# The experts' numbers ahead of the tokens' weights, and another ending of the expert sum, in a transformer block with sixteen experts

## The chip, the cores and the metric

The kernel runs on one core of a Trainium2 chip. The core has five engines with a queue of instructions each: PE (matmul), DVE (vector), ACT (scalar), POOL (GpSimd) and SP, which here only issues DMAs. PE writes to PSUM, the others work between PSUM and SBUF, and 16 DMA engines move data between SBUF and HBM. The metric is the device time of one execution in microseconds.

## The reference

One block: a token mixer (mLSTM heads and a Fourier part), then a mixture of experts with a norm and a residual around it. What the change touches is the end of it.

```python
x = x + gate1 * rmsnorm(y, g_post_mix)
h2 = modulate(rmsnorm(x, g_pre_ffn), shift2, scale2)
x = x + gate2 * rmsnorm(hier_moe(h2), g_post_ffn)

# hier_moe: 512 tokens, 16 experts, each token goes to 2 of one group of 4
for e in range(16):
    a = silu(h @ w_gate[e]) * (h @ w_up[e])
    y = y + combine[..., e, None] * (a @ w_down[e])
```

Tokens have 1024 features, an expert 512 inner ones; everything is float32.

## The kernel before

The mixer takes the first 300 us or so. Then each expert is one column: a list of its tokens is made, the tokens' rows are gathered from a DRAM buffer `h2d`, gate, up and down are applied, the weighted result `yo` is added into the DRAM buffer `ybuf` by an indirect scatter on POOL's queue (L1580). There are 16 columns in the order `SEQ = [0, 1, 2, 11, 3, 8, 4, 12, 5, 9, 6, 13, 7, 10, 14, 15]`. Columns 0 to 2, 14 and 15 hold fixed experts; the eleven between them (3 to 13) are ranked by their number of tokens at run time, so their weights are loaded from an address that SP reads from a small array `idi` of experts' numbers (`values_load`, L1811). `idi` is made on DVE within the routing (L1683 to L1688), behind the first column's code. The routing also makes the tokens' weights in three bf16 parts (L1650 to L1655), sums them by matmuls (`lw`, `lq`) and writes the lists' indices (L1417).

A column takes 12 raw weight tiles of 128x1024 (0.5 MB each), loaded by SP at L1306: 8 for gate and up in four parts, 4 for down. There are 21 raw buffers in rotation (`next_raw`). A heavy column (up to 128 tokens) splits each raw tile in two: ACT casts it to fp32r (`hi`, L1328), DVE takes the rest (`lo`, L1329), and three products hi*hi, lo*hi and hi*lo follow on PE, so 6 matmuls of 128x512 per tile; there are 5 pairs of hi and lo. The raw buffer is free when DVE has its rest. A light column (32 or 64 tokens) multiplies the raw tiles in plain fp32.

`position(n, wsrc)` writes column `SEQ[n]`: `gate_up` with its four parts, and between the parts (the list `mid`) the transposes of the column before, then the turning of the next column's tokens; behind it the `down` of the column before (for the last position, the down of column 14 stands within gate and up, behind part 1). Columns 13, 14, 15 below are named by their place from the end: third from last is column 10 (64 tokens, light), then 14 and 15, heavy both. The prediction calls the third from last "column 13", after its position n = 13.

The ending, `finish(True)`, has three jobs. `ybuf` holds everything but the results of the last two columns, which stay in PSUM (`py`). Each of four blocks of 128 tokens is read from `ybuf` (L1841, on SP), squared and summed on ACT (L1852), multiplied with the gate row `G2` on POOL (704 of 1024 features, L1853) and DVE (L1854), and written to `out` (`w`, L1862 and L1863); tokens of the last two lists are left at the residual there by a zero factor `rest`. For these two lists, rows of `ybuf` are gathered (L1817), the PSUM results are added (`l`, L1870), normed (`p`, L1877), and added into `out` by an indirect scatter (`o`, L1883). A mean square goes through a power on POOL (L1848). `t0` is the down of the last column in three products per tile. The helper `after` chains instructions of one engine in the order of the code, so the order of the ending is that of a string:

```python
ORDER = "s0 s3 w0 t0 s2 l0 w3 s1 w2 w1 l1 p0 p1 o0 o1".split()
```

Elsewhere a scheduler sets the order on each engine, by priorities that follow the code. The helper `mm` at L213 records all matmuls, so PE's rows are told apart by the name of the tile that they write.

## Time and profile before

| | us |
|---|---|
| median of 3 runs | 650.36 (648.5 to 650.47) |
| the profiled execution | 645.57 |
| its span | 643.4 |
| PE busy | 549.3 (85%) |
| DVE busy | 375.3 (58%) |
| ACT busy | 294.8 (46%) |
| POOL busy | 228.0 (35%) |
| DMA moved | 165.24 MB, 257 GB/s in the mean |

The span is the time from the first to the last instruction of the program, the device time also holds what lies around it. Times within rows are us from the span's start, a row of the timeline gives start and duration, and in brackets how long the engine stood idle ahead of it and what ended that. Rows that several instructions share have their count behind an x; back-to-back instructions of one engine overlap by a little, so a row's duration divided by the count is their distance. A row of the stretches gives, behind the stretch and its length, the busy time and the instruction count of PE, PE's weight loads, DVE, ACT and POOL, then the granted PE clock, the busy share of the DMA engines and GB/s.

### The profile page before, as it was taken

The page shows a single profiled execution, that of the slowest core. Times are in us where ns is not written, and L with a number is a line of the kernel's source. Part 1 is how long each engine was busy: PE and PEld are TensorE (multiplying, and loading weights), DVE is VectorE, ACT ScalarE, POOL GpSimd, SP SyncE. Part 2 cuts the span into 40 slices and gives each one's busy share as a digit, 9 for nine tenths or more (in the row PEclk, how much of TensorE's full clock was granted, in tenths as well). Part 3 has the DMA queues.
Part 4 walks back from the last instruction along what each step waited for, and adds up shares of the span by engine and source line. Part 5 has one row for each costly group of instructions (what it writes and reads, how often), then busy time and mean ns, then how long its engine had stood idle before and what let it go on. Part 6 is the DMA issues. An engine that isn't in the chain of part 4 may idle for free. (4 is left out here: it accounts for less than half of the span.)

```text
span 643.4 us, 9141 instructions
## 1 busy us (share of the span) xinstructions
PE 549.3 (85%) x3073; PEld 378.1 (59%) x3073; DVE 375.3 (58%) x692; ACT 294.8 (46%) x478; POOL 228.0 (35%) x264
## 2 busy tenths in 40 slices
PE   3789979699999869997799999999998988998650
PEld 1256855688565647874677766566654555465430
DVE  3560794836247663428999998452735445366780
ACT  2560635443134335224386765462725345367630
POOL 8343940076033346536442236113120010001672
PEclk9989998899999989998799999999999999999875
DMA  8965601131699774256676899999999999998331
GB/s 265 389 253 195 232 0 51 31 99 50 214 318 318 255 310 164 92 189 264 215 275 237 288 387 376 333 389 384 376 389 390 379 387 379 399 383 324 139 132 25
DMA packets 58390, 165.24 MB, mean 257 GB/s; under 512 B 9305, under 2 KB 16757, under 8 KB 58340
## 3 DMA queue, kind: packets, MB, share of 16 engines
q1 hardware_dynamic: 50244, 154.07, 64.2%
q0 software_dynamic: 5536, 10.08, 6.5%
q10 hardware_dynamic: 2560, 0.47, 0.4%
q8 instruction: 25, 0.41, 0.2%
q14 instruction: 25, 0.20, 0.1%
HBM read 154.92 MB, written 15.02 MB: 264 GB/s over the span
## 5 line engine op out<-in xcount | busy, mean ns | idle before, releaser
L1329 DVE TENSOR_TENSOR U<-U,U 128x1024 fp32r<-128x1024 f32 x118 | 141.7, 1248 | 33.8 <-ACT U L1328 33.3
L1328 ACT CAST U<-U 128x1024 fp32r<-128x1024 f32 x118 | 118.4, 1051 | 19.5 <-PE y L213 5.3
L213 PE MATMUL y<-U,U 128*128 128x512 f32 x368 | 100.4, 410 | 10.6 <-ACT U L1510 4.3
L213 PEld LDWEIGHTS y<-U,U 128*128 128x128 f32 x368 | 68.6, 193 | 29.5 <-ACT U L1510 4.5
L213 PE MATMUL gate<-U,U 128*128 128x512 f32 x186 | 55.8, 401 | 5.0 <-DVE U L1329 2.5
L213 PE MATMUL up<-U,U 128*128 128x512 f32 x188 | 56.5, 400 | 1.7 <-ACT U L1328 1.7
L213 PE MATMUL uz<-U,U 128*128 128x512 f32 x192 | 52.4, 409 | 0.2 <-ACT U L603 0.2
L216 POOL TENSOR_TENSOR U<-U,U 128x512 fp32r<-128x512 f32 (+2 forms) x32 | 43.3, 1371 | 4.1 <-ACT U L812 1.5
L213 PEld LDWEIGHTS gate<-U,U 128*128 128x128 f32 x186 | 34.0, 189 | 16.2 <-ACT U L1328 4.8
L213 PEld LDWEIGHTS up<-U,U 128*128 128x128 f32 x188 | 35.0, 189 | 12.1 <-ACT U L1328 3.2
L213 PEld LDWEIGHTS uz<-U,U 128*128 128x128 f32 x192 | 34.9, 189 | 11.9 <-issue 5.5
L213 PE MATMUL gul<-U,U 128*32 128x256 f32 (+1 forms) x296 | 40.4, 442 | 0.0
L1580 POOL DMA_INDIRECT ybuf<-U x8 | 13.9, 1737 | 69.3 <-ACT U L1556 31.6
L1580 POOL DMA_INDIRECT ybuf<-U,U x7 | 11.4, 1628 | 65.5 <-ACT U L1560 47.4
L1335 POOL DMA_INDIRECT U<-h2d,U x16 | 17.6, 1099 | 46.0 <-PE xet L1363 20.4
L213 PE MATMUL win<-U,U 128*128 128x512 f32 x96 | 25.1, 408 | 0.0
L216 DVE TENSOR_TENSOR U<-U,U 128x512 fp32r<-128x512 f32 (+1 forms) x18 | 16.2, 921 | 13.9 <-POOL U L216 9.9
L1490 DVE TENSOR_TENSOR U<-U,up 128x512 f32<-128x512 f32 x10 | 6.9, 686 | 29.8 <-PE up L213 29.8
L1366 DVE TENSOR_TENSOR U<-xet,U 128x512 fp32r<-128x512 f32 x18 | 12.1, 687 | 19.8 <-ACT U L1365 19.8
L213 PEld LDWEIGHTS gul<-U,U 128*32 128x32 f32 (+1 forms) x296 | 14.0, 117 | 15.2 <-issue 9.6
L428 ACT CAST U<-U 128x512 fp32r<-128x512 f32 (+2 forms) x30 | 21.1, 763 | 3.7 <-DMA U<-in_w_in_dram 3.7
L213 PE MATMUL yl<-U,U 128*32 128x256 f32 (+1 forms) x156 | 21.8, 448 | 0.0
(439 smaller groups left out, 1055.7 us busy)
## 6 DMA issues: line engine op xcount, KB each, us to landing
U<-in_w_gate_dram SPq DMA_DIRECT2D x64, 512.0 KB
U<-in_w_up_dram SPq DMA_DIRECT2D x64, 512.0 KB
U<-in_w_down_dram SPq DMA_DIRECT2D x64, 512.0 KB
U<-in_w_ada_dram SPq DMA_DIRECT2D x48, 512.0 KB
U<-in_w_in_dram SPq DMA_DIRECT2D x6, 1024.0 KB
U<-in_w_out_dram SPq DMA_DIRECT2D x4, 1024.0 KB
U<-in_x_dram SPq DMA_DIRECT2D x4, 512.0 KB
x0d<-U SPq DMA_DIRECT2D x4, 512.0 KB
```

The lines of the kernel that those rows point to most:

```text
L213: PE.matmul(out=o, lhsT=l, rhs=r, start=start, stop=stop)
L216: (eng or V).tensor_tensor(o, a, b, op=OP.subtract)
L428: S.copy(hi[:, s], raw[:, s])
L1328: after(S, lambda: S.copy(hi.ap, r.ap))
L1329: after(V, lambda: V.tensor_tensor(lo.ap, r.ap, hi.ap.bitcast(F32), op=OP.subtract))
L1335: g = G.indirect_dma_start(out=xe[0:n], out_offset=None, in_=h2d[:, :], in_offset=bass.IndirectOffsetOnAxis(ap=gi[0:n], axis=0), bounds_ch ...
L1366: V.tensor_tensor(xl[:, s], tp, xh[:, s].bitcast(F32), op=OP.subtract)
L1490: run["mul"] = V.tensor_tensor(sg.ap, sg.ap, p2[1], op=OP.mult)
L1580: run["scatter"] = G.indirect_dma_start(out=to, out_offset=bass.IndirectOffsetOnAxis(ap=gi, axis=0), in_=yo[:, 0:n], in_offset=None, bound ...
```

## The change

It has four parts.

1. In the routing, the instructions that make `idi` stand ahead of those that make the tokens' weights. SP's first register loads of `idi` move with it.
2. The down of the third column from the end is written behind part 1 of column 14's gate and up, not behind all of it. Its four weight loads on SP stand ahead of column 14's parts 2 and 3.
3. The ending begins within the last column: behind part 2 `setup` takes 14 raw buffers, loads `G2`, reads the four blocks of `ybuf`, now on POOL's queue, and gathers the rows of the last two lists; behind part 3 `first` scales two blocks. The multiplication with `G2` is whole on DVE.
4. The last down is in plain fp32 from the raw tiles: one copy of the transposed activations, no splits, 8 matmuls for 24. Then come two more blocks, four writes, and each of the last two lists with its scatter at once behind it. A list's result is multiplied with `G2` while the power is made, and with the power's result afterwards, half on ACT and half on DVE.

```diff
@@ routing, behind the first column
     with tc.issue_after(listed.ins):
-        for w in rw:
-            w()
-        wp, wr_ = ...
-        (the tokens' weights in three bf16 parts, the matmuls lw, parts_sum into ls[:, :, 2])
...
         V.tensor_tensor(ohr, gcol(rank), grow(iota[:, 0:NDYN]), op=OP.is_equal)
-        V.tensor_tensor(t3, ..., op=OP.mult)
-        V.tensor_reduce(lsd, t3, axis=AX.X, op=OP.add)
-        indices(NPRE, NPRE + NDYN, lsd)
         V.tensor_copy(idf, ids)
         V.tensor_tensor(t3[:, :, 0, :], ohr, gcol(ids[:, D_]), op=OP.mult)
         V.tensor_reduce(idf[:, D_], t3[:, :, 0, :], axis=AX.X, op=OP.add)
         idi = idb.ap.bitcast(I32)
         V.tensor_copy(idi, idf)
+        for w in rw:
+            w()
+        wp, wr_ = ...
+        (the same as above)
+        V.tensor_tensor(t3, ..., op=OP.mult)
+        V.tensor_reduce(lsd, t3, axis=AX.X, op=OP.add)
+        indices(NPRE, NPRE + NDYN, lsd)
@@ position(n, wsrc)
         if n == NE - 1:
             mid[1] = lambda: run.update(py=down(pend, box["ya"], keep=True))
+            mid[2:] = [run["setup"], run["first"]]
...
+        if n == NE - 2:
+            mid[1] = lambda: (ahead(), down(pend, box["ya"]))
         s_ = gate_up(tiles, wsrc, run["xs"], mid)
-        if pend is not None and n < NE - 1:
+        if pend is not None and n < NE - 2:
             down(pend, box["ya"], mid=ahead if SEQ[n + 1] == STAR else None)
@@ the ending: new functions, called from position or behind the loop
+    def setup(part):
+        g2 = next_raw()
+        SP.dma_start(out=g2.ap, in_=bc(g2d[:, :], [128, 1024]))
+        fin.update(G2=g2.ap, junk=next_raw(), ys=[next_raw() for _ in range(4)], zs=[next_raw() for _ in range(4)])
+        eng = G if part else SP
+        for tt in range(4):
+            line[eng] = eng.dma_start(out=fin["ys"][tt].ap, in_=ybuf[tt * 128:(tt + 1) * 128, :])
+        if part:
+            fin.update(yg=[next_raw() for _ in LAST], zg=[next_raw() for _ in LAST])
+            for yg, p in zip(fin["yg"], LAST):
+                after(G, lambda: gather(yg.ap, ybuf, iiv[:, p:p + 1], T))
+    def scale(tt, part):
+        y1, y2, c = fin["ys"][tt], fin["zs"][tt], 44 + 4 * tt
+        after(S, lambda: S.activation(fin["junk"].ap, y1.ap, AF.Square, accum_out=st[:, c:c + 1]))
+        inv(c)
+        after(V, lambda: V.tensor_tensor(y2.ap, y1.ap, fin["G2"], op=OP.mult))
...
-            after(G, lambda: G.tensor_tensor(y2[:, 0:NPG], y1[:, 0:NPG], G2[:, 0:NPG], op=OP.mult))
-            after(V, lambda: V.tensor_tensor(y2[:, NPG:1024], y1[:, NPG:1024], G2[:, NPG:1024], op=OP.mult))
...
     def last(i):
...
+        after(V, lambda: V.tensor_tensor(zg.ap, yg.ap, fin["G2"], op=OP.mult))
+    def put(i):
+        zg, r = fin["zg"][i], st[:, 25 + 4 * i:26 + 4 * i]
+        after(S, lambda: S.mul(zg[:, 0:512], zg[:, 0:512], r))
+        after(V, lambda: V.tensor_scalar(zg[:, 512:1024], zg[:, 512:1024], r, None, op0=OP.mult))
+        after(G, lambda: G.indirect_dma_start(out=outv, ..., in_=zg.ap, ..., compute_op=OP.add))
+    def last_products(raws):
+        sg = run["pend"][2][0][0]
+        tp = pT("at")
+        for q in range(4):
+            PE.transpose(tp[:, q * 128:(q + 1) * 128], sg[:, q * 128:(q + 1) * 128], ident)
+        after(S, lambda: S.copy(sg.ap, tp))
+        y = pA("y0"), pA("y1")
+        for kk in range(4):
+            for n in range(2):
+                mm(y[n], sg[:, kk * 128:kk * 128 + 128], raws[kk][:, n * 512:n * 512 + 512], kk == 0, kk == 3)
+        py.append(y)
+    def first():
+        py.append(run["py"])
+        for tt in range(2):
+            scale(tt, True)
@@ behind the last position
-    ahead_of = gate()
-    units = [unit(run["pend"][1], 2, kk) for kk in range(4)]
-    finish(True)      (walks ORDER = "s0 s3 w0 t0 s2 l0 w3 s1 w2 w1 l1 p0 p1 o0 o1")
+    raws = [raw_unit(run["pend"][1], 2, kk) for kk in range(4)]
+    line.update({V: run["mul"], S: run["silu"]})
+    last_products(raws)
+    for tt in range(2, 4):
+        scale(tt, True)
+    for tt in range(4):
+        write(tt)
+    last(0)
+    put(0)
+    last(1)
+    put(1)
```

Line numbers of the changed kernel are two lower than before at the helpers (L1327 for L1329), and differ by more within the routing and the ending.

Part 1 on DVE. Before, in the routing behind the first column (`U_99` is a slot with the routing's small arrays, `lq`, `dup` are PSUM tiles of lists), the cast of the numbers is the last row:

```order
L1679 TENSOR_TENSOR U_99<-U_99 128x363
L1742 COPY U_75<-U_99 128x16
L1366 TENSOR_TENSOR U_1004<-xet,U_2005 128x512
L1681 TENSOR_REDUCE U_99<-U_99 128x33
L1728 COPY U_99<-lq 128x11x2
L1417 SCALAR_TENSOR_TENSOR U_99<-U_99 128x11
L1684 TENSOR_TENSOR U_99<-U_99,U_81 128x11x11
L1707 COPY U_99<-dup 128x9
L1685 TENSOR_REDUCE U_99<-U_99 128x11
L1708 TENSOR_TENSOR U_99<-U_99 128x3
L1644 TENSOR_REDUCE U_99<-lq 128x11
L1688 CAST U_81<-U_99 128x16
```

In the changed kernel the cast is the seventh of these rows, and the 128x1024 row behind it is the split of a raw tile that stood at 333.61 in the trace before:

```order
L1665 TENSOR_TENSOR U_99<-U_99,U_81 128x11x11
L1129 TENSOR_TENSOR U_99<-U_99 128x8
L1415 SCALAR_TENSOR_TENSOR U_99<-U_99 128x2
L1666 TENSOR_REDUCE U_99<-U_99 128x11
L1130 TENSOR_TENSOR U_99<-U_99 128x8
L1741 TENSOR_TENSOR U_99<-U_99 128x16
L1669 CAST U_81<-U_99 128x16
L1131 TENSOR_REDUCE U_99<-U_99 128x2
L1134 SCALAR_TENSOR_TENSOR U_99<-U_99 128x2
L1128 TENSOR_REDUCE U_99<-U_99 128x2
L1327 TENSOR_TENSOR U_1845<-U_1831,U_2425 128x1024
```

The cast stands 35 rows earlier; the index rows of 128x11 (L1417 before, L1415 now) stay behind the tokens' weights.

Part 2 on ACT. Before, at column 14: two casts of its part 1 (the first two rows), its four casts of parts 2 and 3, its silu, the copy of its transposed activations, the light down's result (`yl`), and the casts of column 15.

```order
L1328 CAST U_2425<-U_2421 128x1024
L1328 CAST U_1004<-U_99 128x1024
L1328 CAST U_2005<-U_2427 128x1024
L1328 CAST U_1845<-U_2427 128x1024
L1328 CAST U_2425<-U_2426 128x1024
L1328 CAST U_2425<-U_75 128x1024
L1489 ACTIVATE U_1831<-gate 128x512
L1510 CAST U_1004<-at 128x512
L1556 ACTIVATE U_99<-yl,U_99 128x512
L1328 CAST U_1004<-U_1831 128x1024
L1328 CAST U_2005<-U_81 128x1024
L1328 CAST U_1845<-U_2426 128x1024
```

Now the result of the light down stands ahead of the four casts of parts 2 and 3 (the four rows behind it), and one cast of column 15 ahead of the silu:

```order
L1326 CAST U_2425<-U_2421 128x1024
L1326 CAST U_1004<-U_99 128x1024
L1554 ACTIVATE U_99<-yl,U_99 128x512
L1326 CAST U_2005<-U_1831 128x1024
L1326 CAST U_1845<-U_2006 128x1024
L1326 CAST U_2425<-U_99 128x1024
L1326 CAST U_2425<-U_2427 128x1024
L1326 CAST U_1004<-U_1831 128x1024
L1487 ACTIVATE U_1831<-gate 128x512
L1326 CAST U_2005<-U_81 128x1024
L1326 CAST U_1845<-U_2426 128x1024
L1508 CAST U_1004<-at 128x512
```

What moved is the row with `yl`, from behind the silu to the middle of column 14; all casts of parts 2 and 3 now stand behind it on ACT.

Part 4 on POOL, where the last instructions are. Before, powers and products of the blocks, the power of the last list, and both scatters (`out_dram`) together at the end:

```order
L1848 TENSOR_TENSOR U_75<-U_75 128x1
L1853 TENSOR_TENSOR U_2006<-U_2427,U_99 128x704
L1848 TENSOR_TENSOR U_75<-U_75 128x1
L1858 TENSOR_TENSOR U_75<-U_75,U_99 128x1
L1848 TENSOR_TENSOR U_75<-U_75 128x1
L1883 DMA out_dram<-U_99 512x1024
L1883 DMA out_dram<-U_1831,U_99 512x1024
```

Now the first list's scatter stands between the two lists' powers, and the products with `G2` are gone:

```order
L1832 TENSOR_TENSOR U_75<-U_75 128x1
L1841 TENSOR_TENSOR U_75<-U_75,U_99 128x1
L1832 TENSOR_TENSOR U_75<-U_75 128x1
L1841 TENSOR_TENSOR U_75<-U_75,U_99 128x1
L1832 TENSOR_TENSOR U_75<-U_75 128x1
L1863 DMA out_dram<-U_81,U_99 512x1024
L1832 TENSOR_TENSOR U_75<-U_75 128x1
L1863 DMA out_dram<-U_2426,U_99 512x1024
```

The four reads of `ybuf` stand on this queue as well, ahead of the two gathers, behind the last scatter into `ybuf`.

More of the change, by code (lines that the diff above doesn't have):

```diff
@@ L49 @@
 NXE = 3
-NPG = 704
 RT = 1616
-ORDER = "s0 s3 w0 t0 s2 l0 w3 s1 w2 w1 l1 p0 p1 o0 o1".split()
 NU = 2
@@ L1804, in dyn_w, with gather @@
         return src
+    LAST = NE - 2, NE - 1
+    outv = out.rearrange("o t c -> (o t) c")
+    fin = {}
+    def gather(dst, src, idx, rows):
+        return G.indirect_dma_start(out=dst, out_offset=None, in_=src[:, :], in_offset=bass.IndirectOffsetOnAxis(ap=idx, axis=0),
+                                    bounds_check=rows - 1, oob_is_err=False)
+    def setup(part):
[9 more added lines that the diff above has]
+                after(G, lambda: gather(yg.ap, ybuf, iiv[:, p:p + 1], T))
@@ new lines, in inv @@
+    def inv(c):
+        after(V, lambda: V.tensor_scalar(st[:, c + 2:c + 3], st[:, c:c + 1], 1.0 / D, EPS, op0=OP.mult, op1=OP.add))
+        after(G, lambda: G.tensor_tensor(st[:, c + 1:c + 2], st[:, c + 2:c + 3], mhalf[:, 0:1], op=OP.pow))
+    def scale(tt, part):
[3 more added lines that the diff above has]
+        after(V, lambda: V.tensor_tensor(y2.ap, y1.ap, fin["G2"], op=OP.mult))
+        if part:
+            after(G, lambda: G.tensor_tensor(st[:, c + 1:c + 2], st[:, c + 1:c + 2], rest[:, tt:tt + 1], op=OP.mult))
@@ new lines, in write, with last @@
+    def write(tt):
+        y2 = fin["zs"][tt].ap
+        after(V, lambda: V.scalar_tensor_tensor(y2, y2, st[:, 45 + 4 * tt:46 + 4 * tt], x1[tt].ap, op0=OP.mult, op1=OP.add))
+        after(SP, lambda: SP.dma_start(out=outv[tt * 128:(tt + 1) * 128, :], in_=y2))
+    def last(i):
+        yg, zg, w, c = fin["yg"][i], fin["zg"][i], lists_of(LAST[i])[1], 24 + 4 * i
+        for n in range(2):
+            s = slice(n * 512, n * 512 + 512)
+            after(V, lambda: V.scalar_tensor_tensor(yg[:, s], py[i][n], w, yg[:, s], op0=OP.mult, op1=OP.add))
+            after(S, lambda: S.activation(fin["junk"][:, s], yg[:, s], AF.Square, accum_out=st[:, c + 3 * n:c + 3 * n + 1]))
+        after(V, lambda: V.tensor_tensor(st[:, c:c + 1], st[:, c:c + 1], st[:, c + 3:c + 4], op=OP.add))
+        inv(c)
+        after(V, lambda: V.tensor_tensor(zg.ap, yg.ap, fin["G2"], op=OP.mult))
@@ new lines, in put @@
+    def put(i):
+        zg, r = fin["zg"][i], st[:, 25 + 4 * i:26 + 4 * i]
+        after(S, lambda: S.mul(zg[:, 0:512], zg[:, 0:512], r))
+        after(V, lambda: V.tensor_scalar(zg[:, 512:1024], zg[:, 512:1024], r, None, op0=OP.mult))
+        after(G, lambda: G.indirect_dma_start(out=outv, out_offset=bass.IndirectOffsetOnAxis(ap=iiv[:, LAST[i]:LAST[i] + 1], axis=0),
+                                              in_=zg.ap, in_offset=None, bounds_check=T - 1, oob_is_err=False, compute_op=OP.add))
@@ new lines, in last_products @@
+    def last_products(raws):
[6 more added lines that the diff above has]
+        for kk in range(4):
+            for n in range(2):
+                mm(y[n], sg[:, kk * 128:kk * 128 + 128], raws[kk][:, n * 512:n * 512 + 512], kk == 0, kk == 3)
+        py.append(y)
+    py = []
+    def first():
+        py.append(run["py"])
+        for tt in range(2):
+            scale(tt, True)
@@ L1806, in body @@
+    run.update(setup=lambda: setup(True), first=first)
     for n in range(NPRE, NE):
@@ L1811, in body @@
             position(n, dyn_w(nc.values_load(idi[0:1, c:c + 1], engines=(mybir.EngineType.SP,), min_val=0, max_val=NE - 1)))
-    LAST = NE - 2, NE - 1
-    outv = out.rearrange("o t c -> (o t) c")
-    def gather(dst, src, idx, rows):
-        return G.indirect_dma_start(out=dst, out_offset=None, in_=src[:, :], in_offset=bass.IndirectOffsetOnAxis(ap=idx, axis=0),
-                                    bounds_check=rows - 1, oob_is_err=False)
-    def gate():
-        g2 = next_raw()
-        SP.dma_start(out=g2.ap, in_=bc(g2d[:, :], [128, 1024]))
-        return g2
@@ L1898, in body @@
-    finish(True)
+    raws = [raw_unit(run["pend"][1], 2, kk) for kk in range(4)]
[9 more added lines that the diff above has]
+    put(1)
+    for i in range(2):
+        for n in range(2):
+            s = slice(n * 512, n * 512 + 512)
+            after(S, lambda: S.mul(yob[i][:, s], py[i][n], lists_of(LAST[i])[1]))
     novf = nc.values_load(exiv[0:1, 28:29], min_val=0, max_val=NOV)
@@ L1912, in body @@
             down(gate_up([(lt[:, 0:1], lt[:, 1:2].bitcast(F32))], dyn_w(ev)))
-        finish(False)
+        setup(False)
+        for tt in range(4):
+            scale(tt, False)
+            write(tt)
 _INS = ['x', 'c', 'ctx', 'c_ctx', 'w_ada', 'b_ada', 'g_pre_mix', 'g_post_mix', 'g_pre_ffn', 'g_post_ffn', 'w_in', 'conv_w',
```

83 lines of the change are left out of this document (14 added, 69 removed).

## The prediction

> **What bounds the kernel now.** I read the stretches of the whole span first, then the chain that ended last, then each engine's instructions in time order at the two places that the change touches. Device time is 650.36 us in the median; the profiled execution took 645.57 us with a span of 643.4, so 2.2 us lie around the span. I make the sum against this execution and take the difference over to the median.
>
> Two rows of the stretches show the middle and the far end. In the first both PE and the 16 DMA engines are full; in the second nothing computes.
>
> ```profile
> 440.00:460.00 20.00, 20.00 (x142) 12.19 (x141) 8.81 (x10) 10.14 (x16) 5.81 (x5) 1.00 1.04 393
> 630.00:645.00 15.00, 0.00 (x0) 0.00 (x0) 0.00 (x0) 0.00 (x0) 1.57 (x1) 0.50 0.18 27
> ```
>
> The ending is a serial piece. POOL's last two instructions are the scatters of the last two lists, both of which add into `out`; the second waits until the first has landed. Ahead of them are the last instructions of DVE and PE.
>
> ```profile
> 627.00 2.69 POOL L1883 DMA_INDIRECT out_dram<-U  x1 [0.18 <-issue]
> 635.22 1.57 POOL L1883 DMA_INDIRECT out_dram<-U,U  x1 [5.52 <-DMA out_dram<-U]
> ...
> 603.31 0.69 DVE L1490 TENSOR_TENSOR U<-U,up 128x512 f32<-128x512 f32 x1 [3.85 <-PE up L213]
> 612.75 0.68 DVE L1511 TENSOR_TENSOR U<-at,U 128x512 fp32r<-128x512 f32 x1
> 616.29 1.28 DVE L1862 SCALAR_TENSOR_TENSOR U<-U,U,U 128x1024 f32<-128x1024 f32 x1
> 622.62 1.40 DVE L1870 SCALAR_TENSOR_TENSOR U<-y,U,U 128x512 f32<-128x512 f32 x2
> 625.14 1.27 DVE L1877 SCALAR_TENSOR_TENSOR U<-U,U,U 128x1024 f32<-128x1024 f32 x1
> ...
> 613.48 2.93 PE L213 MATMUL y<-U,U 128*128 128x512 f32 x6 [3.26 <-DVE U L1511]
> 620.91 0.62 PE L213 MATMUL y<-U,U 128*128 128x512 f32 x2
> ```
>
> So the first scatter starts at 627.00, the second 8.22 later, and the span ends 8.18 after that: 16.4 us from the first scatter to the end. The first scatter's own list (column 14) had its products long before; it starts late because both L1877 stand behind the last list's L1870 on DVE, and that needs the last down product on PE (613.48 to 621.5, at half clock), which waited for L1511, which stood behind a write on DVE. The last expert's gate and up are finished when L1490 starts, at 603.31. I call that moment T; before, the first scatter stands at T + 23.7.
>
> **The change, part 1: experts' numbers first.** These rows are DVE and SP where the weights at dynamic addresses begin.
>
> ```profile
> 348.87 0.17 DVE L1688 CAST U<-U 128x16 int32<-128x16 f32 x1
> 351.47 1.21 DVE L1329 TENSOR_TENSOR U<-U,U 128x1024 fp32r<-128x1024 f32 x1
> 356.36 8.08 DVE L1329 TENSOR_TENSOR U<-U,U 128x1024 fp32r<-128x1024 f32 x7
> ...
> SPq L1811 <- DVE U L1688: 5.0, 1, 5.0
> 353.59 0.36 SPq L1306 DMA_DIRECT2D U<-in_w_gate_dram  x1
> 357.75 0.34 SPq L1306 DMA_DIRECT2D U<-in_w_up_dram  x1
> 358.89 0.33 SPq L1306 DMA_DIRECT2D U<-in_w_gate_dram  x1
> ...
> 348.00:350.00 2.00, 1.65 (x16) 0.83 (x15) 1.77 (x17) 0.87 (x2) 1.42 (x2) 1.00 0.06 14
> 358.00:360.00 2.00, 2.00 (x10) 1.64 (x9) 2.00 (x3) 1.35 (x2) 0.00 (x0) 1.00 0.72 209
> ```
>
> SP waits 5.0 us for the numbers, and DMA is nearly idle for a moment. But only the first dynamic load (353.59) hangs on them. The second comes at 357.75, just after the first of the seven L1329 (356.36 + 1.2), the third 1.14 later, one per L1329: they wait for raw buffers, which DVE frees. So the 15 us by which the cast moves up (to about 333.5 by the order below) buy one load. The first load's buffer is freed by the L1329 at 351.47; in the new order most of the list work of 347.3 to 351.4 stands behind it instead of ahead, so I put it at 348 and the load at 349.3, 4 us earlier. The seven L1329 come after the same work less the number's own instructions and less two reductions that waited on PE: about 1.2 us earlier at first, 0.9 after that. Price on SP: two register loads now stand ahead of seven static loads, but the static ones wait for buffers themselves, so about nothing. In DMA work that is some 1.0 us less idle, and as DMA and PE are both full from 362 on, I pass on 1.0 us to T. Bounds: a loss of 1.5 (lists of the third to eleventh column are two microseconds later, and a gather of theirs stands ahead of PE's work), a gain of 3.5 (the idle DMA share from 348 to 358).
>
> **Part 2: column 13's down in the middle of column 14.** Before, ACT stands at the start of the last column behind these products, and PE then behind ACT:
>
> ```profile
> 582.98 1.08 PE L213 MATMUL yl<-U,U 128*64 128x512 f32 x4
> 585.78 0.73 PE L213 MATMUL gate<-U,U 128*128 128x512 f32 x2 [1.72 <-ACT U L1328]
> 587.04 1.20 PE L213 MATMUL gate<-U,U 128*128 128x512 f32 x4 [0.53 <-DVE U L1329]
> 584.10 0.69 ACT L1556 ACTIVATE U<-yl,U 128x512 f32<-128x512 f32 x1 [0.44 <-PE yl L213]
> 585.07 1.55 POOL L1580 DMA_INDIRECT ybuf<-U  x1 [16.41 <-DMA U<-in_w_gate_dram]
> 593.03 1.90 SPq L1841 DMA_DIRECT2D U<-ybuf  x4
> 585.75 13.71 DVE L1329 TENSOR_TENSOR U<-U,U 128x1024 fp32r<-128x1024 f32 x12 [1.36 <-ACT U L1328]
> ```
>
> In the new order L1556's like stands on ACT ahead of column 14's third part, so the same 1.72 + 0.53 come there: the stall moves, and I give this part nothing on PE (bounds: 2.3 gained if it vanishes, 2.3 lost if it comes twice). What moves is the scatter, from 585 to about 577, and with it the reads of `ybuf`, from 593 to about 585.5, since they waited 8 us for its landing. In the same place 14 of 21 raw buffers go to the ending, so the last six weight loads wait for units of the last column: by the row of twelve, the fourth unit is done at 590.3 and the load of part 3 goes out then, where it lands in about 5.7 us (the like on POOL's queue, quoted next); PE wants it, two conversions ahead, at about 598. Hidden, with some 2 us to spare.
>
> **Part 3: the four reads go to POOL's queue.** Two rows disagree on what POOL's transfers cost while DVE streams: a direct one in the middle of seven L1329, and a gather in the middle of the twelve above, which ended 0.9 after them.
>
> ```profile
> 357.04 0.65 POOL L1759 DMA_DIRECT2D lst<-U  x1 [0.32 <-POOL U L1744]
> 593.74 6.67 POOL L1817 DMA_INDIRECT U<-ybuf,U  x1 [7.13 <-PE y L213]
> U<-rowd POOLq DMA_DIRECT2D x3, 512.0 KB, 5.7
> ```
>
> The reads are direct, so I take 0.65 each and 5.7 to landing: all four land by 594, and ACT's first square, which now stands ahead of the silu at 601.88, has its data. The Trainium skill ("SBUF — State Buffer", Who interferes with whom) holds that a transfer issued from GpSimd can be starved by DVE, because it shares a port pair with it, and that a DVE instruction with two SBUF inputs contends with any GpSimd instruction that reads SBUF. By that rule the gather's row would hold for the reads too; it is the second rival below.
>
> **Part 4: the ending from T.** Prices on ACT, POOL and PE (`q` is a plain fp32 product of 128x512 at full clock, 0.43 us each):
>
> ```profile
> 601.88 0.60 ACT L1489 ACTIVATE U<-gate 128x512 f32<-128x512 f32 x1 [4.84 <-PE gate L213]
> 606.15 1.05 ACT L1852 ACTIVATE U<-U 128x1024 f32<-128x1024 f32 x1
> 607.11 0.19 ACT L1852 ACTIVATION_READ_ACCUMULATOR U<-U 128x1 f32 x1
> 611.71 1.52 POOL L1848 TENSOR_TENSOR U<-U 128x1 f32<-128x1 f32 x1
> 604.06 0.65 PE L1501 MATMUL at<-U,U 128*128 128x128 f32 x4 [0.85 <-DVE U L1490]
> 108.64 3.59 PE L213 MATMUL q<-U,U 128*128 128x512 f32 x8
> ```
>
> PE: transposes end at T + 1.4, ACT's copy at T + 2.0, eight fp32 products at T + 5.5 (T + 9 at half clock), in place of four conversions and 24 products. That is early either way, so the last down leaves the path. DVE is the path: L1490, 0.6 from start to start; ACT's squares of the last two row blocks end at T + 3.2 and T + 4.45, so the four products with the gate, now whole on DVE (1.2 each, as L1329), end at T + 5.75; four writes of 1.2 (L1862's row, overlapped), T + 10.55; the two halves of column 14, 1.35, T + 11.9; ACT's second square and two small sums, 1.15; the power on POOL, 1.52, under which DVE multiplies; half a row each on ACT and DVE, 0.6: T + 15.2, and 0.5 to the scatter's start. I add 0.8, since powers on POOL take 0.55 to 1.53 us beside DVE's streams and the fourth write waits for one. First scatter at T + 16.5, against T + 23.7: 7.2 us. The last list needs about 5 us more, while the first scatter takes 8.2 to land, so the second is again bound by the first, and 16.4 us follow.
>
> **Sum.** T = 603.3 - 1.0 = 602.3; first scatter 618.8; end 635.2. That is 8.2 us less; from the median, 642.2 us.
>
> **Rivals.**
> Last weights late: the part 3 loads have 2 us to spare by rows of two different stretches. If they share the DMA engines with six transfers of 0.5 MB (8 us at 390 GB/s), PE waits up to 5 us: 8.2 less 4 gives 646.2. For it: the buffers are really taken; against it: the reads start at 585.5, ahead of them. The same place holds if the stall of part 2 comes twice.
> Reads held (the other side): POOL's reads wait as the gather did. If all are let go at the stream's end (599.5), the first lands at 605.8, ACT's silu moves from 601.9 to 607.1, and the sum shrinks by 5.2 to 3.0: 647.4. If each of the four is held 6.67 in turn, the last lands near 618, its square, product and write end near 621.7 and the first scatter stands at 627.7: 651.1, slower. It turns at about 6.5 us per read.
> A larger gain: the stall of 2.25 vanishes, or part 1 brings its 3.5: 11 us less, 639.4.
> Part 1 doing nothing is inside my forecast: 643.2.
>
> **Chances.** Forecast 0.57 (own range 640.5 to 644.5), last weights late 0.15, reads held 0.13 (0.08 let go together, 0.05 each in turn), larger gain 0.15. The range takes the larger gain with its bounds (12.4 less) and the reads let go together (2.4 less): 638.0 to 648.0. A change under 0.3%, 2 us, can't be told from none here. Of the late weights 0.04 and of the reads let go together 0.03 may come so low; the reads held in turn are the slower case. Faster 0.88, same 0.07, slower 0.05.
>
> **What would show it.** Right: the cast of the numbers near 333.5, the first dynamic load near 349 but the second still after 356; POOL's reads near 586, under 1 us each; PE's 2.25 us stall inside column 14; the first scatter about 16.5 us after the last mul of gate and up, the second 8 us behind. Wrong: a silu on ACT that waits for a read of `ybuf`, PE waiting for the last gate or up weights, or a second scatter that starts late for its own list.

## The result, and the profile after

The changed kernel takes 641.67 us in the median of four runs, the kernel before 650.41 beside it: a ratio of 0.987, 95% interval 0.9829 to 0.9912. The forecast was 642.2. The profiled execution of the changed kernel took 642.93 us with a span of 641.2.

The two profiled executions can't be subtracted as they stand. These are rows of the kernel before: the end of the first list's making on DVE (L1417, code that the change does not touch) and four products of column 14's second unit on PE, which wait 0.53 us for DVE in every version of this kernel.

```profile
323.89 0.15 DVE L1417 SCALAR_TENSOR_TENSOR U<-U 128x3 int32<-128x3 f32 x1
566.81 1.20 PE L213 MATMUL gate<-U,U 128*128 128x512 f32 x4 [0.53 <-DVE U L1329]
```

The same two places in the changed kernel stand first in the next fence (lines have moved by two), then in order of time the last mul of gate and up (T), the last down on PE, DVE's writes and the first list's sums, and the two scatters.

```profile
328.07 0.15 DVE L1415 SCALAR_TENSOR_TENSOR U<-U 128x3 int32<-128x3 f32 x1
571.86 1.19 PE L211 MATMUL gate<-U,U 128*128 128x512 f32 x4 [0.53 <-DVE U L1327]
609.84 0.69 DVE L1488 TENSOR_TENSOR U<-U,up 128x512 f32<-128x512 f32 x1 [0.31 <-PE up L211]
611.92 7.13 PE L211 MATMUL y<-U,U 128*128 128x512 f32 x16 [0.67 <-ACT U L1872]
616.54 3.67 DVE L1845 SCALAR_TENSOR_TENSOR U<-U,U,U 128x1024 f32<-128x1024 f32 x3
620.13 1.40 DVE L1853 SCALAR_TENSOR_TENSOR U<-y,U,U 128x512 f32<-128x512 f32 x2
624.24 0.49 DVE L1862 TENSOR_SCALAR U<-U,U 128x512 f32<-128x512 f32 x1 [0.44 <-POOL U L1832]
625.56 1.68 POOL L1863 DMA_INDIRECT out_dram<-U,U  x1 [1.35 <-DVE U L1853]
632.61 1.60 POOL L1863 DMA_INDIRECT out_dram<-U,U  x1 [3.81 <-ACTq L1911]
```

Unchanged code ended at 323.89 in the one and at 328.07 in the other: 4.2 us that belong to the execution, not to the change. So I cut the span at five moments and compare stretches: A, the first list (first row); B, the four products (second row); T; S1 and S2, the starts of the two scatters; the end. Column A is the start of its row, the others are differences of two such row starts; the end is the span, which is known to 0.1 us.

| kernel | A | A to B | B to T | T to S1 | S1 to S2 | S2 to end |
|---|---|---|---|---|---|---|
| before | 323.89 | 242.92 | 36.50 | 23.69 | 8.22 | 8.18 |
| changed | 328.07 | 243.79 | 37.98 | 15.72 | 7.05 | 8.59 |
| numbers only | 325.51 | 244.07 | 36.53 | 23.70 | 7.86 | 8.13 |
| changed, no numbers | 323.16 | 244.62 | 37.93 | 15.72 | 7.08 | 8.59 |
| changed, scatters last | 324.88 | 243.70 | 38.04 | 18.84 | 6.83 | 8.51 |
| changed, down in three products | 324.15 | 243.35 | 37.97 | 19.55 | 6.84 | 8.54 |
| changed, down 13 late | 325.46 | 242.22 | 36.77 | 15.72 | 7.04 | 8.59 |
| changed, reads on SP | 324.82 | 242.77 | 37.08 | 15.72 | 7.10 | 8.11 |
| weighting late | 324.52 | 243.81 | 36.52 | 15.73 | 7.20 | 8.52 |
| + last weights first | 326.43 | 243.92 | 33.86 | 15.71 | 7.15 | 8.53 |
| + all blocks early | 325.90 | 243.35 | 35.40 | 10.99 | 7.03 | 8.53 |
| + first list ahead | 323.52 | 243.30 | 35.35 | 13.74 | 7.03 | 8.56 |
| before, order alone | 325.10 | 243.27 | 36.56 | 23.35 | 6.90 | 8.22 |
| before, gate row on DVE | 325.49 | 243.99 | 38.11 | 23.72 | 8.06 | 8.23 |

From B on the kernel before takes 76.6 us, the changed one 69.3. These 7.3 us are an ending that is 8.7 shorter (40.1 to 31.4) and a last column that is 1.5 longer. T to S1 repeats within 0.02 us where the code from T on is the same (15.71 to 15.73 in six kernels), the whole ending within 0.5 us (30.9 to 31.5 in the same six), while A alone moves by 4.9 us between executions; where the medians below can't tell, the stretches often can.

### The profile page after: what moved, and what is told of

It reads as the page before. It is cut to its first block, busy times and chain, and to the rows that moved or that the text cites. A ratio compares the mean times of both kernels' runs of the same rounds, so it can differ in the third digit from the quotient of the medians.

```text
span 641.2 us, 9108 instructions
## 1 busy us (share of the span) xinstructions
PE 554.6 (86%) x3065; PEld 381.4 (59%) x3065; DVE 368.2 (57%) x689; ACT 292.4 (46%) x476; POOL 222.1 (35%) x264
## 4 chain that ended last, share of the span: by engine, by line
PE 43%; DMA 27%; DVE 11%; issue 6%; POOL 6%; ACT 5%; POOLq 0%; SPq 0%; ACTq 0%; DVEq 0%
DMA U<-in_w_gate_dram 8%; PE y L211 8%; DMA U<-in_w_down_dram 6%; PE up L211 5%; PE gate L211 4%; PE uz L211 4%; DMA U<-in_w_up_dram 3%; PE gul L211 2%; DMA U<-in_w_ada_dram 2%; PE ada2p L838 2%; PE win L211 2%; DMA U<-in_w_in_dram 2%; PE num L211 2%; DMA U<-h2d,U 2%; PE ada1p L211 2%
## 5 line engine op out<-in xcount | busy, mean ns | idle before, releaser
L1327 DVE TENSOR_TENSOR U<-U,U 128x1024 fp32r<-128x1024 f32 x114 | 135.6, 1232 | 43.4 <-ACT U L1326 34.1
L1326 ACT CAST U<-U 128x1024 fp32r<-128x1024 f32 x114 | 114.8, 1051 | 24.0 <-PE pos L211 6.8
L211 PE MATMUL y<-U,U 128*128 128x512 f32 x368 | 102.0, 418 | 3.3 <-ACT U L1326 1.9
L211 PE MATMUL up<-U,U 128*128 128x512 f32 x188 | 57.9, 405 | 2.8 <-ACT U L1326 1.7
L211 PEld LDWEIGHTS uz<-U,U 128*128 128x128 f32 x192 | 34.9, 189 | 11.9 <-issue 5.5
L1333 POOL DMA_INDIRECT U<-h2d,U x16 | 19.5, 1222 | 50.3 <-PE xet L1361 19.9
L211 PE MATMUL gate<-U 128*128 128x512 f32 x54 | 20.5, 410 | 3.3 <-ACT U L1326 2.7
L211 PEld LDWEIGHTS gul<-U,U 128*32 128x32 f32 (+1 forms) x296 | 14.0, 117 | 15.1 <-issue 9.8
```

The lines of the kernel that those rows point to most:

```text
L211: PE.matmul(out=o, lhsT=l, rhs=r, start=start, stop=stop)
L1326: after(S, lambda: S.copy(hi.ap, r.ap))
L1327: after(V, lambda: V.tensor_tensor(lo.ap, r.ap, hi.ap.bitcast(F32), op=OP.subtract))
L1333: g = G.indirect_dma_start(out=xe[0:n], out_offset=None, in_=h2d[:, :], in_offset=bass.IndirectOffsetOnAxis(ap=gi[0:n], axis=0), bounds_ch ...
```

## The experiments

### Part 1 alone, and everything but part 1

```diff
 with tc.issue_after(listed.ins):      (numbers only: the kernel before with this order)
+    (numbers of the experts into idi)
     (tokens' weights, lw, parts_sum)
-    (numbers of the experts into idi)
```

> The kernel before with part 1 alone (the experts' numbers ahead of the tokens' weights). Theory: nothing, 650 us (ratio 0.998 to 1.002): only the first load at a dynamic address moves up, by about 4 us, and what it gains is gone before the middle, where in the two profiles the loads stood at the same time (566.50 after, 562.33 before, with 4.18 us already between them before the routing). The prediction: 1.0 us faster, ratio 0.9985. Rival: the idle DMA share from 348 to 358 is really filled, 2 to 3.5 us faster, ratio 0.995 to 0.997.

> The changed kernel without part 1 (routing in its old order). Theory: the whole gain stays, ratio 0.987 to before (about 641.7 us), and from the last mul of gate and up to the end of the span it takes the same 31.4 us as in the changed kernel. The prediction: 1.0 us slower than the changed kernel, ratio 0.9885. Rival: part 1 delays the last column (its last mul stood 2.35 us later than aligned), then this one is 1 to 2 us faster than the changed kernel, ratio 0.984.

Measured: part 1 alone 0.9975 (0.9945 to 1.0005), everything but part 1 0.9876 (0.9833 to 0.9919). The first interval holds no change, the prediction's 1.0 us and a gain of 3 alike. The stretch from A to B decides little more: it is 242.2 to 244.1 us in the ten kernels with part 1 and 242.9 to 244.6 in the four without it, 243.4 and 243.7 in the mean. There is no gain of 2 us in it, and one of 1.0 can't be told from none. How it is lost is seen on SP. Rows of part 1 alone, the first two loads from dynamic addresses and the eighth and ninth:

```profile
351.82 0.36 SPq L1306 DMA_DIRECT2D U<-in_w_gate_dram  x1
358.84 0.34 SPq L1306 DMA_DIRECT2D U<-in_w_up_dram  x1
...
366.53 0.33 SPq L1306 DMA_DIRECT2D U<-in_w_up_dram  x1
370.43 0.33 SPq L1306 DMA_DIRECT2D U<-in_w_gate_dram  x1
```

and the ninth before:

```profile
366.53 0.33 SPq L1306 DMA_DIRECT2D U<-in_w_gate_dram  x1
```

With the 1.62 us between the two A taken off, the first load went out 3.4 us earlier than before (350.20 for 353.59), the second 0.5 earlier, and the ninth 2.3 later (368.81 for 366.53). Counted from A and in the mean over all kernels of the table, the second load goes out 1.3 us earlier with part 1 than without it, the third and the eighth 0.4 us earlier, and the ninth 1.0 later (368.0 to 368.8 in the ten kernels with it, 366.5 to 368.2 in the four without). The loads wait for raw buffers; having the address early advances little more than one load. Why the ninth comes later is not shown.

### Column 13's down, and the weighting on ACT

In the changed kernel the stall that stood at the start of the last column before stands within column 14. Rows of the changed kernel: ACT's weighting of `yl`, PE's two waits and the units behind them, and the stretch from the end of `yl` to column 14's last product.

```profile
582.67 0.69 ACT L1554 ACTIVATE U<-yl,U 128x512 f32<-128x512 f32 x1 [7.97 <-PE yl L211]
584.34 0.50 PE L211 MATMUL gate<-U 128*128 128x512 f32 x1 [1.71 <-ACT U L1326]
585.60 0.74 PE L211 MATMUL gate<-U 128*128 128x512 f32 x2 [0.53 <-DVE U L1327]
586.71 2.76 PE L211 MATMUL up<-U,U 128*128 128x512 f32 x6
582.60:592.40 9.80, 7.56 (x26) 5.72 (x26) 5.77 (x5) 6.63 (x8) 2.02 (x2) 0.83 0.60 213
```

The waits are 1.71 and 0.53, as before (1.72 and 0.53). Behind them six products took 2.76 us, nearly twice the 1.53 of other units, with a granted clock of 0.83 in the stretch (0.50 from 586.7 to 589.7). Then two experiments: the down back where it was, and the weighting behind all casts of column 14.

```diff
 (down 13 late)
-        if n == NE - 2:
-            mid[1] = lambda: (ahead(), down(pend, box["ya"]))
-        if pend is not None and n < NE - 2:
+        if pend is not None and n < NE - 1:
 (weighting late)
-                S.mul(yo[:, 0:n], py[0][:, 0:n], two[1])      (for column 13: put off)
+    def weigh():      (behind part 3 of column 14's gate and up)
+        after(S, lambda: S.mul(yo[:, 0:n], p[:, 0:n], two[1]))
+        held.append((yo, two[0], n)); release(1)
```

> The changed kernel without part 2: column 13's down behind all of column 14's gate and up, as before. In the traces the way from column 14's second gate unit to the last mul of gate and up took 36.5 us before and 38.0 in the changed kernel. Theory: it is 36.5 again, the reads of ybuf go out 6 to 8 us later (when column 13's scatter has landed, some 26 us after that gate unit) but still land ahead of the last mul, and the ending keeps its 31.4 us: 1.5 us faster than the changed kernel, ratio 0.985 to before. Rival, the reason that the diff suggests for part 2: the late reads hold the squares on ACT and with them the ending, by 2 to 5 us: ratio 0.990 to 0.995.

> The changed kernel with one instruction of ACT moved: the weighting of column 13's result (128x512 from PSUM) stands behind all eight casts of column 14 instead of in the middle of them, where ACT stood idle 7.97 us for the products yl. Theory: PE's two waits in column 14 (1.71 and 0.53 us) vanish and with them the slow stretch behind them (four units of six products took 9.8 us from the end of yl, at 0.227 us each they need 5.5): 3 to 4.3 us faster than the changed kernel, ratio 0.981 to before, about 638. Rival: the last two weight tiles of the last column, which ACT awaited 2.68 us, land no earlier, and the time is that of the changed kernel: ratio 0.987.

Measured: down 13 late 0.9813 (0.9769 to 0.9857), weighting late 0.9825 (0.9784 to 0.9865). B to T is 36.77 and 36.52 us against 37.98, and T to S1 is the same 15.7 in both. So part 2 isn't needed in this kernel: without it the reads of `ybuf` go out 23.4 us after B instead of 20.1 and are early enough.

```profile
591.10 2.26 POOL L1821 DMA_DIRECT2D U<-ybuf  x4 [3.60 <-DVE U L1327]
593.67 5.38 POOL L1811 DMA_INDIRECT U<-ybuf,U  x1 [0.30 <-issue]
604.45 0.69 DVE L1488 TENSOR_TENSOR U<-U,up 128x512 f32<-128x512 f32 x1 [0.16 <-ACT U L1834]
```

The late weighting did what was expected on PE: from the end of `yl` (579.0) to the start of column 15's products (584.6) 5.6 us for four units, against 9.7 in the changed kernel. But T gained 1.5 instead of 3 to 4.3, because the rival was there too. ACT of the kernel with the late weighting:

```profile
579.12 0.69 ACT L1570 ACTIVATE U<-yl,U 128x512 f32<-128x512 f32 x1 [4.14 <-PE yl L211]
598.64 1.05 ACT L1326 CAST U<-U 128x1024 fp32r<-128x1024 f32 x1 [4.38 <-DMA U<-in_w_gate_dram]
601.19 1.05 ACT L1326 CAST U<-U 128x1024 fp32r<-128x1024 f32 x1 [1.50 <-DMA U<-in_w_up_dram]
```

The last two weight tiles are late there: they wait for raw buffers that the ending has taken. The next kernel loads them first.

### The last weights before the ending's buffers

```diff
-            mid[2:] = [run["setup"], run["first"]]
+            def part3():
+                for kind in range(2):
+                    early[kind, 3] = load(wsrc, kind, 3); rawb.pop()
+                run["setup"]()
+            mid[2:] = [part3, run["first"]]
```

> The kernel with the late weighting (0.9825 of before) and one thing more: the last column's part 3 weights are loaded before the ending takes its 14 raw buffers. In that kernel ACT waited 4.38 and 1.50 us for these two tiles, which went out at 589.86 and 591.00 and landed behind the four reads of ybuf, and PE waited 0.49 + 0.53 + 0.52 in the same stretch. Theory: those waits vanish, the last mul comes 1.5 to 2 us earlier, and the ending keeps its 31.4 us: ratio 0.980. Rival: two loads earlier means the reads of ybuf or the last down's tiles later by as much, and nothing is gained: 0.9825.

Measured: 0.9822 (0.9777 to 0.9868), which alone shows nothing against 0.9825. The trace does: the two tiles go out at 581.29 and 582.58, ACT's nine casts run in one piece, and B to T is 33.86, 2.7 us less than with the late weighting alone.

```profile
581.29 0.33 SPq L1304 DMA_DIRECT2D U<-in_w_gate_dram  x1
582.58 0.33 SPq L1304 DMA_DIRECT2D U<-in_w_up_dram  x1
589.65 8.64 ACT L1326 CAST U<-U 128x1024 fp32r<-128x1024 f32 x9
```

This is the prediction's first rival, found in the trace and taken away. In the changed kernel itself it cost nothing visible: PE was behind its own stall, and the cast that ACT's wait for these tiles held up ended at 605.77, 1.1 us before PE's products of that tile began (606.85):

```profile
604.72 1.05 ACT L1326 CAST U<-U 128x1024 fp32r<-128x1024 f32 x1 [2.68 <-DMA U<-in_w_gate_dram]
```

### The reads on SP

```diff
-        eng = G if part else SP
+        eng = SP
```

> The changed kernel with the four reads of ybuf on SP's queue in place of POOL's; the last column's part 3 weights and the last down's tiles then stand behind them on SP. Theory: part 3 of the change is worth about nothing: on POOL the four reads took 2.26 us together and were not held, and on SP they go out at the same time, when column 13's scatter has landed (some 20 us behind column 14's second gate unit), while the weights behind them wait for raw buffers until about then anyway: ratio 0.987 as the changed kernel, last mul within 1 us. Rival: SP's queue is what the change protects, the last weights go out 2 us later or more and the last mul with them: ratio 0.990 or above.

Measured: 0.9855 (0.9817 to 0.9894), T to S1 15.72 as in the changed kernel, B to T 37.08, 0.9 less than in the changed kernel and still 0.6 more than before. Here the stall of 1.71 and 0.53 is as in the changed kernel, yet the six products behind it ran at full speed (granted clock 1.00), so that the dip in the clock is worth about 1.2 us in those six alone, and comes or stays away. Rows on SP and PE:

```profile
586.98 1.75 SPq L1823 DMA_DIRECT2D U<-ybuf  x4
582.34 1.53 PE L211 MATMUL up<-U,U 128*128 128x512 f32 x6
```

A worth of the reads' queue, either way, is not seen in these stretches: what differs in B to T is of the size of the dip.

### What the ending's 8 us are made of

Four kernels take one piece each away from the changed kernel or add one to the kernel before.

```diff
 (scatters last: the changed kernel with)
-    last(0); put(0); last(1); put(1)
+    last(0); last(1); put(0); put(1)
 (down in three products: the changed kernel with)
-    last_products(raws)
+    units = [unit(run["pend"][1], 2, kk) for kk in range(4)]
+    ya = turn_a(run["pend"]); py.append(down(run["pend"], ya, keep=True, units=units))
 (order alone: the kernel before with)
-ORDER = "s0 s3 w0 t0 s2 l0 w3 s1 w2 w1 l1 p0 p1 o0 o1".split()
+ORDER = "s0 s3 w0 t0 s2 l0 w3 s1 w2 w1 p0 o0 l1 p1 o1".split()
 (gate row on DVE: the kernel before with)
-            after(G, lambda: G.tensor_tensor(y2[:, 0:NPG], ...))
-            after(V, lambda: V.tensor_tensor(y2[:, NPG:1024], ...))
+            after(V, lambda: V.tensor_tensor(y2.ap, y1.ap, G2, op=OP.mult))
```

> The changed kernel with the first list's scatter behind the last list's sums: DVE and ACT take both lists up to the product with the gate, then both are multiplied and scattered. Theory: the first scatter starts 3 us later (19 us instead of 15.7 after the last mul of gate and up; ahead of it on DVE come two halves of 0.7, a small sum that waits for ACT's square, and a product of 1.2), the second follows 7 to 8 us behind, so 3 us are lost: ratio 0.992 to before. Rival: the order of the two lists costs nothing, because the first one's landing waits for the writes: ratio 0.987.

> The changed kernel with the last down in three fp32r products again (four casts on ACT, four remainders of 1.2 us and one of 0.7 on DVE, 24 products), everything else as in the changed kernel. Theory: the fp32 down pays on DVE, not on PE: the five remainders stand on DVE between the last mul of gate and up and the scaling of blocks 2 and 3, so the first scatter starts 4 x 1.2 + 0.7 = 5.5 us later (21.2 us after that mul instead of 15.7) and the end follows: ratio 0.995 to before. Rival: PE's products decide (24 fp32r of 0.227 us for 8 fp32 that took 7.13): 1.7 us faster or no change, ratio 0.984 to 0.987.

> The kernel before with two letters of its order moved: the first list's product and scatter stand ahead of the last list's sums (w1 p0 o0 l1 p1 o1), nothing else. Theory: of the 8 us of the ending this is the part that the order alone brings: the first list's product starts on DVE at 622.6 instead of 625.1, the first scatter 2.6 us earlier (21.1 behind the last mul instead of 23.7), the second 8 behind it: ratio 0.996. Rival: the last list is then the bound (its product ends about 7 us after the first scatter's start), second scatter not earlier: ratio 1.000.

> The kernel before with one thing changed: the product with the gate row is whole on DVE (four of 1.2 us for four of 0.48), and POOL's four of 1.7 us are gone; order, last down and reads as before. Theory: POOL's share cost more than it took over: before, two of the writes on DVE took 2.68 and 2.76 us beside POOL's products for 1.28 alone, and DVE waited 0.68 and 0.71 for POOL; that is 4.2 us against 2.9 more on DVE, so the last write ends 1.3 us earlier and the first scatter with it (22.4 behind the last mul for 23.7): ratio 0.998. Rival: DVE is the bound of that stretch and POOL only stands beside it, first scatter 1.5 to 3 us later: ratio 1.002 to 1.005. Second rival: POOL was the bound, first scatter 4 us earlier: ratio 0.994.

Measured: scatters last 0.9909 (0.9876 to 0.9942), down in three products 0.9914 (0.9883 to 0.9944), order alone 0.9979 (0.9951 to 1.0008), gate row on DVE 1.001 (0.9978 to 1.0041).

Scatters last loses 3.1 us from T to S1 and gets 0.3 back afterwards: as expected. With the down in three products the four remainders and one more stand between T and the scaling, as expected. They take 5.1 us, and a wait of 1.22 us for ACT that DVE has there in the changed kernel (ahead of 612.94) lies beneath them, so 3.8 us are lost instead of 5.5. DVE and POOL rows of the kernel with the down in three products:

```profile
607.27 4.62 DVE L1327 TENSOR_TENSOR U<-U,U 128x1024 fp32r<-128x1024 f32 x4
611.81 0.68 DVE L1509 TENSOR_TENSOR U<-at,U 128x512 fp32r<-128x512 f32 x1
...
625.02 1.68 POOL L1863 DMA_INDIRECT out_dram<-U,U  x1 [1.35 <-DVE U L1853]
```

So the fp32 down pays on DVE. On PE it is the slower form: 7.13 us for its 8 products at a granted clock of 1.00, where 24 in fp32r at the pace of column 14's undisturbed units (six in 1.36 us from start to start) would be 5.4.

Order alone missed for the first scatter. The first list's product moved up as expected, but the scatter only from 23.69 to 23.35 us after T. The second scatter did gain: it follows 6.90 us behind the first for 8.22, and the whole ending is 38.5 us against 40.1 before and 39.7 with part 1 alone. So in the kernel before the order is worth 1.2 to 1.6 us, which the median (0.9979, no change inside its interval) can't tell from none. Rows of that kernel, the last write and the product on DVE, and the scatter:

```profile
623.06 1.28 DVE L1862 SCALAR_TENSOR_TENSOR U<-U,U,U 128x1024 f32<-128x1024 f32 x1 [0.71 <-POOL U L1858]
624.26 1.28 DVE L1877 SCALAR_TENSOR_TENSOR U<-U,U,U 128x1024 f32<-128x1024 f32 x1
628.28 1.68 POOL L1883 DMA_INDIRECT out_dram<-U  x1 [5.25 <-DVE U L1847]
```

The product is done at 625.54, and the scatter starts 2.7 us later. It does not wait for DVE to be free, which stands idle from 626.85 to 627.70. What is left to wait for is the last write's landing: the scatter adds into rows that the writes fill, and it starts 3.94 us after the last write's end on DVE (624.34). The 16 DMA engines move their last bytes at 626.8, 1.5 us before the scatter. For the second scatter, whose wait the profile does put down to the DMA, it is the same: last bytes at 633.7, start at 635.18. Rows of the kernel before, the last write on DVE and the power of the last list on POOL, which stands ahead of both scatters in that order:

```profile
621.42 1.28 DVE L1862 SCALAR_TENSOR_TENSOR U<-U,U,U 128x1024 f32<-128x1024 f32 x1 [0.71 <-POOL U L1858]
625.30 1.52 POOL L1848 TENSOR_TENSOR U<-U 128x1 f32<-128x1 f32 x1 [3.91 <-DVE U L1847]
```

There the last write ended at 622.70 and its last bytes moved at 625.2, which with 1.5 us gives a landing at 626.7; the first list's product ended at 626.41, and POOL's power for the last list at 626.82, 0.18 before the scatter. So the first scatter before stood behind three chains that ended within 0.4 us of each other: the list's product, the landing of the writes and POOL's power. The order moved the first and the third, and the landing held the scatter. That it waits for the landing is inferred from these intervals; the profile names a small row on DVE at that place. The kernel with the first list ahead, below, shows the same interval.

Gate row on DVE missed too, by all three theories: T to S1 is 23.72. What I said of the single rows holds; writes that took 2.68 and 2.76 us beside POOL's products took 1.29 and 1.28. The first two rows are of the kernel before, the others of this one:

```profile
610.15 2.68 DVE L1862 SCALAR_TENSOR_TENSOR U<-U,U,U 128x1024 f32<-128x1024 f32 x1 [0.68 <-POOL U L1858]
617.95 2.76 DVE L1862 SCALAR_TENSOR_TENSOR U<-U,U,U 128x1024 f32<-128x1024 f32 x1
...
615.89 1.29 DVE L1861 SCALAR_TENSOR_TENSOR U<-U,U,U 128x1024 f32<-128x1024 f32 x1 [0.68 <-POOL U L1857]
623.74 1.28 DVE L1861 SCALAR_TENSOR_TENSOR U<-U,U,U 128x1024 f32<-128x1024 f32 x1
625.73 1.29 DVE L1861 SCALAR_TENSOR_TENSOR U<-U,U,U 128x1024 f32<-128x1024 f32 x1 [0.71 <-POOL U L1857]
```

That is 2.9 us saved, and the four longer products cost 4 x 0.74 = 3.0. The waits of 0.68 and 0.71 that I counted to POOL's products are for its powers, and stayed. So in the kernel before, where the product with the gate row is made was worth nothing.

### Two versions beyond the change

With the waits before T gone, ACT and DVE have room for all four blocks ahead of the last mul (all blocks early), and then the first list's sums could go ahead of the writes (first list ahead). Both stand on the kernel with the last weights first.

```diff
 (all blocks early)
-        for tt in range(2):
+        for tt in range(4):      (in first, ahead of silu and mul of the last column)
             scale(tt, True)
-    for tt in range(2, 4):
-        scale(tt, True)
 (first list ahead: the same, and)
+    last(0)
     for tt in range(4):
         write(tt)
-    last(0)
     put(0)
```

> The same, and all four blocks of ybuf (not two) are squared on ACT and multiplied with the gate row on DVE behind the last column's part 3 and ahead of its silu and mul. Theory: in the 15.7 us from the last mul to the first scatter DVE has two products of 1.2 less and one wait of 1.2 for ACT less; the powers on POOL (four, 1.65 to 2.2 us from start to start) then bound the writes. First scatter 5 to 8 us earlier than in the kernel with the late weighting, the second still 7.1 behind it: ratio 0.970 to 0.975. Rival: the squares delay the silu and mul by as much as they save (DVE and ACT are the bound, not the waits), ratio 0.980 to 0.9825.

> The kernel with all four blocks early (0.9736 of before), and the first list's sums stand on DVE ahead of the four writes instead of behind them, so that ACT's squares and POOL's power for that list lie under the writes. Theory: DVE decides between the last mul and the first scatter; its waits of 0.79 and 0.44 us and the product of 1.2 with its power go under the writes: first scatter 2 us earlier (9 instead of 11 us behind the last mul), second again 7.0 behind it: ratio 0.970 to 0.971. Rival: the first scatter then waits for the writes to land, or for POOL's four powers, and moves by less than 0.7 us: ratio 0.9735.

Measured: all blocks early 632.21 us, 0.9736 (0.9691 to 0.9781), the best of all kernels and below both of the pair; first list ahead 0.9834 (0.9796 to 0.9872). DVE and POOL of all blocks early, the last product with the gate row, the writes, the scatters:

```profile
603.52 1.21 DVE L1855 TENSOR_TENSOR U<-U,U 128x1024 f32<-128x1024 f32 x1
605.25 5.04 DVE L1862 SCALAR_TENSOR_TENSOR U<-U,U,U 128x1024 f32<-128x1024 f32 x4
615.64 1.68 POOL L1880 DMA_INDIRECT out_dram<-U  x1 [1.35 <-DVE U L1870]
622.67 1.60 POOL L1880 DMA_INDIRECT out_dram<-U,U  x1 [3.79 <-ACTq L1926]
```

The mul comes 1.5 us later, behind four products instead of one, and the scatter 4.7 earlier after it: B to S1 is 46.4 us, against 52.2 with the late weighting and 53.7 in the changed kernel. First list ahead fell for the reason that its rival names, and lost rather than stood still:

```profile
606.84 4.87 DVE L1862 SCALAR_TENSOR_TENSOR U<-U,U,U 128x1024 f32<-128x1024 f32 x4
611.62 0.48 DVE L1879 TENSOR_SCALAR U<-U,U 128x512 f32<-128x512 f32 x1
615.91 1.68 POOL L1880 DMA_INDIRECT out_dram<-U  x1 [8.58 <-DVE U L1874]
```

The list was ready at 612.1, and the scatter started at 615.91, 4.2 us after the last write's end (611.71) and 1.4 after the last bytes on the DMA engines (614.5). Putting work ahead of the writes delays their landing, and that is what the first scatter waits for. Its median is 5.2 us above that of all blocks early, where the table has 2.8 us; its six runs reach from 633.35 to 640.11, and what makes the rest is not shown.

## Why the prediction was right, point by point

The time was right, 642.2 for 641.67, but that it is right to 0.5 us is luck. The terms add up to 8.2 us less; from B on the stretches give 7.3, and the two medians 8.7 with an interval from 5.7 to 11.1. Some of the terms miss, and in part they cancel. By the stretches:

- Part 1, 1.0 us: not found, though the stretch from A to B can't rule it out. The cast of the numbers and the first dynamic load came where the prediction had put them, as the rows of the changed kernel show with 4.18 us taken off (333.7, 349.3):

```profile
337.90 0.16 DVE L1669 CAST U<-U 128x16 int32<-128x16 f32 x1
352.08 1.23 DVE L1327 TENSOR_TENSOR U<-U,U 128x1024 fp32r<-128x1024 f32 x1
353.44 0.36 SPq L1304 DMA_DIRECT2D U<-in_w_gate_dram  x1
360.77 0.34 SPq L1304 DMA_DIRECT2D U<-in_w_up_dram  x1
```

  The step that failed is "about 1.2 us earlier at first, 0.9 after that", and with it "I pass on 1.0 us to T": the second load came 1.3 us earlier in the mean, the third only 0.4, and by the ninth nothing was left. The prediction had part 1 doing nothing as a case inside its forecast, 643.2.
- Part 2, nothing: the stall moved, as said, with the same 1.71 + 0.53. Unforeseen was the half clock behind it. B to T became 1.5 us longer, and 0.6 longer in the one kernel with the stall there and no dip (reads on SP), so 0.9 to 1.5 of it go to the dip. It came in four of the five kernels with the stall within column 14 and in one of five with the stall at the last column's start (gate row on DVE, 38.11), so that it belongs to the stall's place is possible and not shown.
- Part 3, hidden and not held: right. Four reads in 2.26 us on POOL, and no difference by the queue was seen. The rival of the held reads did not occur.
- Part 4, first scatter at T + 16.5: it came at T + 15.72. The path on DVE came as it was added up (writes done at T + 10.4 for 10.55, the first list's halves at T + 11.7 for 11.9, its scaling at T + 15.1 for 15.2); the 0.8 that was added for the powers on POOL was not needed. The second scatter was given the 8.22 us of before and took 7.05, and the end took 0.4 more: 16.4 us after the first scatter became 15.6.
- The price of the last down was misread by a factor of two. The row of `q` has eight records, but the code makes four products there (one per head), so a plain fp32 product of 128x512 is two records and took some 0.9 us at full clock, not 0.43. The eight products took 7.13 us at a granted clock of 1.00 and ended at T + 9.2, where the prediction had T + 5.5 at full clock. It cost nothing, since the last list's sums on DVE come to them only at T + 14.8; the prediction's case of T + 9, which it gave to half clock, covered it by luck.
- The reason given for the late first scatter, that the first list's product stood behind the last list's sums, was half of it. The writes' landing was as late, and order alone brought 0.34 us there (and 1.0 to 1.3 us between the scatters, which the prediction did not count). The forecast held because the new ending shortened all of these chains: its last write ends 10.4 us after T (616.54 + 3.67) instead of 19.4.
- The last weights: "some 2 us to spare" was about 1.1 in the changed kernel; as soon as the stall ahead of them was gone they were the wait.
- The range from 638.0 to 648.0 can't be redone to the tenth: its ends stand for 12.4 and 2.4 us less, where the stated terms give 8.2 + 2.25 + 2.5 = 12.95 and 8.2 - 5.2 = 3.0. The measured time lies well inside either way.

Of the ending's 8.7 us, taking back the order costs 2.8 (40.1 to 31.4 in the changed kernel, 34.2 with scatters last) and taking back the fp32 down 3.6 (34.9); the place of the gate row, tried in the kernel before, and the queue of the reads showed no worth. The pieces need not add up, since several chains meet at the first scatter: the order alone was worth 1.2 to 1.6 us in the kernel before. The remaining 2 us or so, two blocks scaled before T and four writes in one piece, were not taken apart one by one.

## What to carry to other kernels

When several chains meet in one last instruction, list the end of each before moving one: an accumulate into rows that plain writes fill waits for the slowest write to land (here some 4 us after DVE was done), and that may be hidden just beneath the chain one is looking at. An instruction that waits long on an in-order engine (here 7.97 us on ACT for one 0.69 us weighting) should stand behind the work that others wait for, not ahead of it. Judge a change of 1% by stretches between fixed instructions, since unchanged code ahead of them may move more than that.

## What the runs showed of the hardware that was not expected

- Code that was the same in all kernels ended between 323.16 and 328.07 us (A in the table), 0.8% of the whole time.
- The first scatter's own time on POOL is 2.67 to 2.69 us where a DVE product of 128x1024 with its inputs in SBUF runs in it (before, numbers only, gate row on DVE), and 1.65 to 1.68 in the other kernels; the second follows after 7.9 to 8.2 us in the first group and 6.8 to 7.2 in the second. DVE's writes took 2.68 and 2.76 us beside POOL's products and 1.28 without them. The Trainium skill ("SBUF — State Buffer", Who interferes with whom) says that a DVE instruction with two inputs in SBUF contends with a GpSimd instruction that reads SBUF; the rows agree for POOL's products.
- For direct reads issued from POOL no hold was seen, so the hold that the prediction's second rival lays on them by that section did not come: in the kernel with the late weighting four went out beside seven remainders on DVE, at 0.57 us each.

```profile
588.13 2.26 POOL L1834 DMA_DIRECT2D U<-ybuf  x4 [6.52 <-DVE U L1327]
588.61 8.04 DVE L1327 TENSOR_TENSOR U<-U,U 128x1024 fp32r<-128x1024 f32 x7 [0.19 <-ACT U L1326]
```

- The first gather, which took 6.67 us before, took 5.38 with the down late, 2.43 in the kernel with the gate row on DVE and 1.1 to 2.1 in the others with the new ending, and DVE streamed beside it there as well; what holds it stays open.
